# Two-layer encoder trunk on one core: the half of a step's projection pieces that stood between its scores and its transpositions is listed behind the transpositions

## The chip, the core and the metric

The kernel runs on one core of a Trainium2 chip. The metric is the device time of one execution in microseconds. Three runs of the kernel before gave 2654.55, 2655.66 and 2656.12 us; their median, 2655.66 us, is the time before. Lower is better. A difference is called faster or slower here if it is more than 0.2% of that, some 5.3 us.

The engines in the profile are PE (matrix multiplication), PEld (its loading of the stationary operand), DVE (vector), ACT (scalar and activation functions), POOL (a second, slower vector engine) and SP, which only issues transfers (SPq in a timeline).

## What is computed

One sequence of 2048 positions with 1024 channels goes through a gated layer A and then an attention layer B. Only layer B is touched. Its query block of 64 positions sees its own block of 64 and the eight before it:

```python
q, z = jnp.split(h @ w_qz, 2, axis=-1)
...
sc = jnp.einsum('bqhd,bkhd->bhqk', qc, kc).astype(jnp.float32) + bias
...
p = jax.nn.softmax(sc, axis=-1).astype(vc.dtype)
return jnp.einsum('bhqk,bkhd->bqhd', p, vc)
...
return (o * jax.nn.silu(z)) @ w_out
```

There are 16 heads of 64 channels, and `k` and `v` are projections of the same stream. The residual is added to the result and a last normalisation follows.

## The kernel before

**Staging.** The first part of the program (to about 1536 us of the profile) is layer A and the projection of all values; it is not touched. The second part is layer B. Positions are cut into four tiles of 512 (`t` from 0 to 3), and heads are taken two at a time (`p` from 0 to 7), so there are 32 pairs. For each pair there are eight steps `u`: two heads with four query blocks of 128 rows each.

**What a step of attention does.** `score(t, p, u)` multiplies a query block with up to 640 keys on PE into the one two-bank tile of the pool `bss` (names `s`); DVE adds the bias, keeps the maximum and moves the sum out of that tile (L1406); ACT takes the exponential and the row sum (L1413); DVE takes the reciprocal (L1416); POOL scales the row (L1417). `flip(t, p, u)` transposes the scaled block on PE, up to five 128x128 blocks, into the one two-bank tile of the pool `ptr` (names `tp`); ACT copies it out as the high part (L1437), and DVE subtracts that from the same tile to get the low part (L1438). Both go into `pt`, of which there is one buffer. `value(t, p, hd)` multiplies the four transposed blocks of a head with the values (16 matmuls named `pv`, 8 in tile 0). Scores run ahead: in step `u` the scores of step `u + 2` are made, in the last two steps those of the next pair.

**Projection pieces.** Between these stand pieces of other PE work, which a generator `ahead(t, p)` hands out: the projections of queries, keys and gate for the next pair (`project`, `values`, `gate`), and from tile 1 on pieces of the output projection of the tile before (`outs`). All multiplications with weights run as three matmuls, high by high, low by high and high by low, at L111, L112 and L113. A piece is three of them; they are named `pj` for the projections and `bo` for the output projection. Both accumulate in the four-buffer pool `pmm`, which `value` uses too. Each projection of 24 matmuls needs its weights split by ACT (L228) and DVE (L229) ahead of it. `steps_of(t, p)` says how many pieces a pair has (16 to 32, with 24 to 30 from tile 1 on in most pairs), and `total * (2 * u + 1) // per` and `total * (2 * u + 2) // per` say how many are to have been handed out by the middle and by the end of step `u`.

**What sets the order.** The listed order is not the order of the instructions on the engines. A scheduler goes through the list and may take a later instruction first when by its own account an earlier one isn't ready; each engine then runs its queue in the order so made, and waits on semaphores. What stands in a queue is therefore read from the built program.

The loop of a step, lines 1909 to 1931, reads in short:

```python
for u in range(8):
    score(...)                                 # of two steps later
    take(gen, upto - done)                     # pieces, first half
    if u == 4: value(t, p, 0)
    elif u == 0 and before: value(*before, 1)
    flip(t, p, u)
    ...                                        # drains, stores, squares
    take(gen, upto - done)                     # pieces, second half
```

Of the kernel before, what the change touches and what calls it, by code (L numbers as in the profile page):

```python
# [33 lines left out]
def trunk_kernel(  # L34
# [224 lines left out]
    def o_right(t):  # L259
        def right(ph):  # L260
            if (t, ph) in o_early:
                return o_early.pop((t, ph))
            out = []
            for q in range(2):
                name = f"bo{t}_{ph}_{q}"
                w = [w_tile(f"w{i}_{name}") for i in "hl"]
                if ph in o_raw:
                    raw = raw_w(1, f"raw_{name}")
                    nc.sync.dma_start(raw[:], wb_out[o_raw[ph]][q])
                    hi = split_in(raw, *w)  # L270
                    if (ph, q) == (1, 1):
                        on_beat(hi)
                else:
                    for i in range(2):
                        nc.sync.dma_start(w[i][:].bitcast(F32), ows[ph, q][:, i, :])
                out.append(w)
            return out
        return right
# [1000 lines left out]
    with ExitStack() as bctx:  # L1279
# [16 lines left out]
        def half_tile(tag, name, bufs, dtype=F32):  # L1296
            return sb.tile([P, 512], dtype, tag=tag, name=name, bufs=bufs)
# [17 lines left out]
        def project(t, p):  # L1315
            for acc in one(t, p, 1):
                yield
            for hd in range(2):
                qh = sb.tile([P, T], F32R, tag="Q", name=f"Qh{t}_{p}_{hd}", bufs=8)
                ql = sb.tile([P, T], F32R, tag="Q", name=f"Ql{t}_{p}_{hd}", bufs=8)  # L1320
                r, r2 = halves(hd)
                nc.scalar.mul(qh[r, :], acc[r, :], 0.125)
                nc.vector.scalar_tensor_tensor(
                    ql[r, :], acc[r, :], 0.125, qh[r, :].bitcast(F32),
                    op0=ALU.mult, op1=ALU.subtract,
                )
                for x_ in (qh, ql):
                    nc.sync.dma_start(x_[r2, :].bitcast(F32), x_[r, :].bitcast(F32))
                qt[t, p, hd] = (qh, ql)
            for acc in one(t, p, 0):  # L1330
                yield
            for hd in range(2):
                r, r2 = halves(hd)
                kx = sb.tile([P, 2 * T], F32R, tag="K", name=f"K{t}_{p}_{hd}", bufs=4)
                nc.scalar.copy(kx[r, T:], acc[r, :])
                nc.vector.tensor_tensor(
                    kx[r2, T:], acc[r, :], kx[r, T:].bitcast(F32), op=ALU.subtract
                )
                if t + 1 < NT:
                    k_store = (khd[t][p][hd], kx[:, T:].bitcast(F32))  # L1340
                    if held:
                        kept.append(k_store)
                    else:
                        nc.sync.dma_start(*k_store)
                if t > 0:
                    nc.sync.dma_start(kx[:, :T].bitcast(F32), khd[t - 1][p][hd])
                kt[t, p, hd] = kx
            if not held:
                keep_all()
# [116 lines left out]
        def drain_all():  # L1466
            while drains:
                drains.pop(0)()
# [28 lines left out]
        def square_all(every=False):  # L1497
            if every:
                squares.extend(young)
                young.clear()  # L1500
            while squares:
                on_beat(squares.pop(0)())
            squares.extend(young)
            young.clear()
# [9 lines left out]
        def send_all():  # L1514
            while owed_out:
                on_beat(nc.sync.dma_start(*owed_out.pop(0)))
# [39 lines left out]
        def last_open():  # L1556
            big = [sh.tile([P, 4, 1024], F32, tag=f"h{i}", name=f"A_h{i}") for i in "hl"]
            for i, n in enumerate(("00", "10", "01", "11", "s3", "s1", "s2", "s4")):
                la[n] = big[i // 4][:, i % 4, :]
            for c, k in ((0, 4), (1, 2)):  # L1560
                for r in range(2):
                    nc.sync.dma_start(
                        la[f"{r}{c}"][:, : k * 256],
                        ogd[NT - 1][:, r, 4 * c : 4 * c + k].rearrange("p k j s -> p (k j s)"),
                    )

            def third():
                for cs in (slice(0, 512), slice(512, 1024)):
                    on_beat(tg(la["s3"][:, cs], la["00"][:, cs], la["10"][:, cs], op=sub))

            def all_of(cs):
                for f_ in last_sums(cs):
                    f_()

            return [lambda: None, third] + last_sums(slice(0, 512)) + [lambda: all_of(slice(512, 768))]
# [250 lines left out]
        def take(gen, n):  # L1826
            for _ in range(n):
                if next(gen, gen) is gen:
                    return

        def run(gen):
            for _ in gen:
                pass
# [16 lines left out]
        def ahead(t, p):  # L1850

            if t > 1 and p == 0:
                next(outs[t - 1])
            if p + 1 < NPAIR:
                yield from project(t, p + 1)
                values(t, p + 1)
                for q in GATES[t][p]:
                    yield from gate(t, q)
                if (t, p) == (1, 4):
                    next(outs[0])  # L1860
                yield from some(outs[t - 1], SHARE[t][p])
            elif t + 1 < NT:
                yield from some(outs[t - 1], SHARE[t][p])
                yield from border(t)
                yield from project(t + 1, 0)
                values(t + 1, 0)
                yield from gate(t + 1, 0)
            else:
                yield from some(outs[t - 1], SHARE[t][p] - 6)
                last_first()  # L1870
                yield from some(outs[t - 1], 6)
                yield from some(outs[t], 13)

        def steps_of(t, p):
            n = 24
            if p + 1 < NPAIR:
                n = 16 + 8 * len(GATES[t][p])
            elif t + 1 == NT:
                n = 13
            return n + SHARE[t][p]  # L1880

        load_bias(0, 0)
        gen = project(0, 0)
# [9 lines left out]
        for t in range(NT):  # L1893
            for p in range(NPAIR):
                gen = ahead(t, p) if t + p else first
                total = steps_of(t, p) - (0 if t + p else 8)
                per = 11 if p + 1 == NPAIR and t + 1 < NT else 16
                todo = []
                if t + 1 == NT and p + 1 == NPAIR:
                    o_early[t - 1, 3] = o_right(t - 1)(3)  # L1900
                    todo = last_open()
                if t == 1 and p < 4:
                    todo = o_sums(p, lambda n: half_tile("C", n, 4), lambda n: half_tile(
                        "S", n, 4, F32R
                    ))
                if (t, p) == (0, 3):
                    nc.sync.dma_start(gf[:], fin_g.partition_broadcast(P))
                done = 0
                for u in range(8):
                    if u < 6:  # L1910
                        score(t, p, u + 2)
                    elif p + 1 < NPAIR or t + 1 < NT:
                        score(t + (p + 1) // NPAIR, (p + 1) % NPAIR, u - 6)
                    upto = total * (2 * u + 1) // per
                    take(gen, upto - done)
                    done = max(done, upto)
                    if u == 4:
                        value(t, p, 0)
                    elif u == 0 and before:
                        value(*before, 1)  # L1920
                    flip(t, p, u)
                    drain_all()
                    send_all()
                    square_all()
                    if u and finals:
                        finals.pop(0)()
                    if todo:
                        todo.pop(0)()
                    upto = total * (2 * u + 2) // per
                    take(gen, upto - done)  # L1930
                    done = max(done, upto)
                if t + 1 < NT or p + 1 < NPAIR:
                    run(gen)
                before = t, p
# [61 lines left out]
```

## Time and profile before

| | |
|---|---|
| median of three runs | 2655.66 us |
| span of the profiled execution, first to last instruction | 2652.0 us |
| run median less span | 3.7 us |
| PE busy in the span | 2608.0 us (98%) |
| DVE busy | 1885.1 us (71%) |
| ACT busy | 1303.2 us (49%) |
| POOL busy | 897.2 us (34%) |
| mean granted PE clock | 0.996 |

The profiled execution is known by its span alone; no time of its own around the span is listed for it, so the distance of 3.7 us between span and median is taken as what lies around it. A row of a group reads: line, engine, operation, output and inputs, shape and count, then busy time and the mean time of one, then the idle time of the engine just ahead of these instructions and what ended most of it. A row of a timeline reads: start and length in us, engine, line, operation, output and inputs, and in brackets the idle time ahead with what ended it. A row of stretches gives for each engine its busy time, then the granted clock of PE, the share of the transfer engines, and their rate.

### The profile page before, as it was taken

What the parts mean: (1) busy time and instruction counts of PE and PEld (TensorE: products, weight loads), DVE (VectorE), ACT (ScalarE), POOL (GpSimd) and SP (SyncE); (2) the same over time, 40 slices, a digit from 0 to 9 for tenths busy, and PEclk for the clock granted to TensorE, in tenths of its full rate; (3) what the DMA queues carried; (4) which work ended last, traced back from release to release, by engine and by line L of the source; (5) the groups of instructions that cost most, each with busy time, mean ns of one, the idle gap of its engine ahead of it and who ended that gap; (6) DMA issues with size and microseconds to landing.
All of it is one profiled execution on the core that took longest, in us unless ns stands there. A gap on an engine that the chain in (4) does not pass through costs nothing. (4 is left out here: it accounts for less than half of the span.)

```text
span 2652.0 us, 37980 instructions
## 1 busy us (share of the span) xinstructions
PE 2608.0 (98%) x12960; PEld 2181.4 (82%) x12960; DVE 1885.1 (71%) x2944; ACT 1303.2 (49%) x2303; POOL 897.2 (34%) x874
## 2 busy tenths in 40 slices
PE   8999999999999999999989999999999999999997
PEld 7888888888888888888878878888888888888886
DVE  5655676865767667757767767777778777877677
ACT  5422243442533434343356456666666655666564
POOL 3611334142152322203234434344332232332245
PEclk9999999999999999999999999999999999999999
DMA  7898998989989869967776597778787666875667
GB/s 286 313 344 329 346 370 323 323 323 338 330 302 313 308 233 324 331 206 270 280 251 214 186 280 229 231 245 263 252 270 254 226 204 224 255 230 161 195 224 251
DMA packets 273856, 718.72 MB, mean 271 GB/s; under 512 B 28800, under 2 KB 68736, under 8 KB 273664
## 3 DMA queue, kind: packets, MB, share of 16 engines
q1 hardware_dynamic: 273664, 716.31, 78.4%
q8 instruction: 103, 1.69, 0.3%
q14 instruction: 89, 0.73, 0.1%
HBM read 531.12 MB, written 174.59 MB: 266 GB/s over the span
## 5 line engine op out<-in xcount | busy, mean ns | idle before, releaser
L111 PE MATMUL P<-T,S 128*128 128x512 f32 x1248 | 496.2, 398 | 2.1 <-ACT S L434 2.1
L112 PE MATMUL P<-T,S 128*128 128x512 f32 x1248 | 488.2, 391 | 1.1 <-DVE T L437 1.1
L113 PE MATMUL P<-T,S 128*128 128x512 f32 x1248 | 488.6, 391 | 0.0
L1417 POOL TENSOR_SCALAR pr<-pr,sl 128x640 f32<-128x640 f32 (+4 forms) x256 | 209.7, 819 | 530.4 <-DVE sl L1416 445.2
L111 PE MATMUL pj<-hh_b,wh_b 128*128 128x512 f32 x768 | 320.4, 417 | 0.0
L113 PE MATMUL pj<-hh_b,wl_b 128*128 128x512 f32 x768 | 305.0, 397 | 1.2 <-DVE wl_b L229 1.1
L112 PE MATMUL pj<-hl_b,wh_b 128*128 128x512 f32 x768 | 303.4, 395 | 0.1
L1413 ACT ACTIVATE pr<-pr,nm 128x640 f32<-128x640 f32 (+4 forms) x256 | 195.5, 764 | 188.1 <-DVE nm L1406 186.6
L113 PEld LDWEIGHTS P<-T,S 128*128 128x128 f32 x1248 | 234.9, 188 | 50.5
L111 PEld LDWEIGHTS P<-T,S 128*128 128x128 f32 x1248 | 235.5, 189 | 46.9 <-ACT S L434 2.3
L112 PEld LDWEIGHTS P<-T,S 128*128 128x128 f32 x1248 | 235.6, 189 | 46.1 <-DVE T L437 1.3
L1438 DVE TENSOR_TENSOR pt<-tp,pt 128x640 fp32r<-128x640 f32 (+4 forms) x256 | 188.4, 736 | 43.7 <-ACT pt L1437 41.1
L1406 DVE CUSTOM_DVE_ANT_0 pr<-s,bias 128x640 f32<-128x640 f32 (+4 forms) x256 | 187.9, 734 | 35.7 <-PE s L1398 29.8
L1437 ACT CAST pt<-tp 128x640 fp32r<-128x640 f32 (+4 forms) x256 | 159.0, 621 | 54.0 <-PE tp L1433 49.8
L1433 PE MATMUL tp<-ident,pr 128*128 128x128 f32 x1120 | 166.7, 275 | 8.6 <-DVE pt L1438 7.3
L113 PEld LDWEIGHTS pj<-hh_b,wl_b 128*128 128x128 f32 x768 | 144.7, 188 | 36.4 <-DVE wl_b L229 3.8
L1433 PEld LDWEIGHTS tp<-ident,pr 128*128 128x128 f32 x1120 | 130.7, 140 | 43.3 <-issue 13.7
L111 PEld LDWEIGHTS pj<-hh_b,wh_b 128*128 128x128 f32 x768 | 145.8, 190 | 18.1 <-ACT wh_b L228 1.6
L1458 PEld LDWEIGHTS pv<-pt,V 128*128 128x128 f32 x896 | 143.3, 189 | 20.8 <-DVE pt L1438 3.9
L112 PEld LDWEIGHTS pj<-hl_b,wh_b 128*128 128x128 f32 x768 | 145.8, 190 | 17.1 <-DVE hl_b L186 0.6
L1458 PE MATMUL pv<-pt,V 128*128 128x256 f32 (+3 forms) x896 | 154.5, 320 | 2.2 <-ACT pt L1437 1.1
L229 DVE TENSOR_TENSOR wl_b<-raw_b,wh_b 128x1024 fp32r<-128x1024 f32 x96 | 120.4, 1255 | 28.5 <-ACT wh_b L228 27.8
(294 smaller groups left out, 5725.9 us busy)
## 6 DMA issues: line engine op xcount, KB each, us to landing
S<-hsd SPq DMA_DIRECT2D x288, 512.0 KB, 5.3
rw<-in_w_a SPq DMA_DIRECT2D x108, 512.0 KB, 6.3
A<-ytd SPq DMA_DIRECT2D x72, 512.0 KB, 5.7
raw_b<-wk SPq DMA_DIRECT2D x72, 512.0 KB, 4.3
hsd<-S SPq DMA_DIRECT2D x56, 512.0 KB, 4.9
V<-vhd SPq DMA_DIRECT2D x56, 512.0 KB, 5.4
bias<-reld SPq DMA_DIRECT2D x64, 320.0 KB, 4.2
va<-vd SPq DMA_DIRECT2D x32, 512.0 KB, 5.5
```

Source lines behind the costliest of these rows:

```text
L111: first = mm(ps, lh, rh, start=first, stop=False)
L112: mm(ps, lh, rl, start=False, stop=False)
L113: mm(ps, ll, rh, start=False, stop=last)
L229: tv(wl[:], raw[:], wh[:].bitcast(F32), op=sub)
L1406: nc.vector.tensor_tensor_reduce(out=pr[:, c0:].rearrange("p (a b) -> p a b", a=nseg), in0=ps[:, :nseg, :w], in1=bias[:, c0:].rearrange("p ...
L1413: nc.scalar.activation(pr[:, c0:], pr[:, c0:], AF.Exp, scale=-1.0, bias=nm[:], accum_out=sl[:])
L1417: nc.gpsimd.tensor_scalar(pr[:, c0:], pr[:, c0:], sl[:], 1.0, op0=ALU.mult, op1=ALU.mult)
L1433: ins = tpose(tp[:, b, :], pr[:, b * P : (b + 1) * P], ident[:])
L1437: nc.scalar.copy(oh, tp[:, b0:5, :].rearrange("p a b -> p (a b)"))
L1438: nc.vector.tensor_tensor(pt[:, 2560 + o + b0 * P : 2560 + o + 640], tp[:, b0:5, :].rearrange("p a b -> p (a b)"), oh.bitcast(F32), op=ALU ...
L1458: mm(po[:, q0 * P : q1 * P], vtl[t, p][:, i, hs], rhs, start=(i == blocks[0] and j == 0), stop=(i == 7 and j == 1),)
```

## The change

Three lines go. The first of the two calls of `take` in a step is left out, so nothing is handed out between the scores and the transpositions; the call at the end of the step, which is unchanged, then hands out all that is due by the end of the step. The number of pieces by the end of each step stays the same.

```diff
                     elif p + 1 < NPAIR or t + 1 < NT:
                         score(t + (p + 1) // NPAIR, (p + 1) % NPAIR, u - 6)
-                    upto = total * (2 * u + 1) // per
-                    take(gen, upto - done)
-                    done = max(done, upto)
                     if u == 4:
                         value(t, p, 0)
                     elif u == 0 and before:
                         value(*before, 1)
                     flip(t, p, u)
```

No instruction is added or removed; 3522 of some 12960 matmuls stand at another place of PE's queue, all of them in layer B. Three places show how.

**PE, tile 2, heads 4 and 5, the middle of a pair.** `s_4_3` are the scores of head 4, block 3; `tp_4_1` is the transposition of head 4, block 1; `pj_3_1` is the query projection of the next pair. Before:

```order
L1398 MATMUL s_4_3_20110<-K_2_0_19853,Qh_2_0_19766 128x320 x2
L1398 MATMUL s_4_3_20110<-K_2_0_19853,Ql_2_0_19767 128x320 x2
L111 MATMUL pj_3_1_20067<-hh_b,wh_b_3_1_20062 128x512
L112 MATMUL pj_3_1_20067<-hl_b,wh_b_3_1_20062 128x512
L113 MATMUL pj_3_1_20067<-hh_b,wl_b_3_1_20063 128x512
L111 MATMUL pj_3_1_20067<-hh_b,wh_b_3_1_20062 128x512
L112 MATMUL pj_3_1_20067<-hl_b,wh_b_3_1_20062 128x512
L113 MATMUL pj_3_1_20067<-hh_b,wl_b_3_1_20063 128x512
L1433 MATMUL tp_4_1_20128<-ident,pr_4_1_19995 128x128 x5
```

The same place of the changed program:

```order
L1398 MATMUL s_4_3_20110<-K_2_0_19883,Qh_2_0_19774 128x320 x2
L1398 MATMUL s_4_3_20110<-K_2_0_19883,Ql_2_0_19775 128x320 x2
L1433 MATMUL tp_4_1_20122<-ident,pr_4_1_19995 128x128 x5
L111 MATMUL pj_3_1_20100<-hh_b,wh_b_3_1_20095 128x512
L112 MATMUL pj_3_1_20100<-hl_b,wh_b_3_1_20095 128x512
L113 MATMUL pj_3_1_20100<-hh_b,wl_b_3_1_20096 128x512
```

The transposition moved ahead of six projection matmuls, to the scores; behind it now stand twelve in a run.

**PE, the border of tile 1 and tile 2.** `tp_15_3` is the last transposition of tile 1, `pv_15` the product of that head with its values, `s_0_1` and `s_0_2` are scores of tile 2. Before:

```order
L1398 MATMUL s_0_1_19211<-K_0_0_19143,Ql_0_0_19045 128x320 x2
L1433 MATMUL tp_15_3_19226<-ident,pr_15_3_19113 128x128 x5
L111 MATMUL pj_1_1_19267<-hh_b,wh_b_1_1_19262 128x512
L112 MATMUL pj_1_1_19267<-hl_b,wh_b_1_1_19262 128x512
L113 MATMUL pj_1_1_19267<-hh_b,wl_b_1_1_19263 128x512
L111 MATMUL pj_1_1_19267<-hh_b,wh_b_1_1_19262 128x512
L112 MATMUL pj_1_1_19267<-hl_b,wh_b_1_1_19262 128x512
L1398 MATMUL s_0_2_19238<-K_0_0_19143,Qh_0_0_19044 128x320 x2
L1398 MATMUL s_0_2_19238<-K_0_0_19143,Ql_0_0_19045 128x320 x2
L1458 MATMUL pv_15_19271<-pt_15_19086,V_7_18522 128x512
```

In the changed program:

```order
L1398 MATMUL s_0_1_19211<-K_0_0_19137,Ql_0_0_19075 128x320 x2
L1433 MATMUL tp_15_3_19223<-ident,pr_15_3_19113 128x128 x5
L1458 MATMUL pv_15_19246<-pt_15_19054,V_7_18522 128x512
L111 MATMUL pj_1_1_19296<-hh_b,wh_b_1_1_19291 128x512
L1398 MATMUL s_0_2_19234<-K_0_0_19137,Qh_0_0_19074 128x320 x2
L1398 MATMUL s_0_2_19234<-K_0_0_19137,Ql_0_0_19075 128x320 x2
L112 MATMUL pj_1_1_19296<-hl_b,wh_b_1_1_19291 128x512
L1458 MATMUL pv_15_19246<-pt_15_19054,V_7_18522 128x512 x3
```

The first `pv` matmul follows the transposition at once, where five projection matmuls and a block of scores stood between them.

**DVE, the same pair of tile 2 as at first.** `nm` and `pr` are written by the reduction that empties the tile of scores (L1406, two rows each), `pt_4` with `tp_4_2` by the subtraction that empties the transposition's tile (L1438), `wl_b_3_0` is the low part of the key weights (L229). Before:

```order
L1406 ISA pr_5_0_20147,nm_5_0_20148<-s_5_0_20142,bias_5_19986 128x640
L1406 ISA nm_5_0_20148 128x1
L229 TENSOR_TENSOR wl_b_3_0_20171<-raw_b_3_0_20169,wh_b_3_0_20170 128x1024
L1416 RECIPROCAL sl_5_0_20149<-sl_5_0_20149 128x1
L1406 ISA pr_5_1_20202,nm_5_1_20203<-s_5_1_20197,bias_5_19986 128x640
L1406 ISA nm_5_1_20203 128x1
L1323 SCALAR_TENSOR_TENSOR Ql_3_0_20158<-pj_3_1_20067,Qh_3_0_20157 64x512
L1438 TENSOR_TENSOR pt_4_20088<-tp_4_2_20179,pt_4_20088 128x640
```

In the changed program:

```order
L1406 ISA pr_5_0_20147,nm_5_0_20148<-s_5_0_20142,bias_5_19986 128x640
L1406 ISA nm_5_0_20148 128x1
L1438 TENSOR_TENSOR pt_4_20078<-tp_4_2_20154,pt_4_20078 128x640
L1406 ISA pr_5_1_20202,nm_5_1_20203<-s_5_1_20197,bias_5_19986 128x640
L1406 ISA nm_5_1_20203 128x1
L1416 RECIPROCAL sl_5_0_20149<-sl_5_0_20149 128x1
L1323 SCALAR_TENSOR_TENSOR Ql_3_0_20166<-pj_3_1_20100,Qh_3_0_20165 64x512
L229 TENSOR_TENSOR wl_b_3_0_20179<-raw_b_3_0_20177,wh_b_3_0_20178 128x1024
```

The subtraction moved ahead of the weight split and of a query split, and stands right behind the reduction.

## The prediction

> **What bounds the kernel now.** I read the totals of the engines first, then four stretches of the span, then PE's waits in the stretches that the change touches, then its groups of instructions. The totals:
>
> ```profile
> span 2652.0 us, 37980 instructions
> PE 2608.0 (98%) x12960; PEld 2181.4 (82%) x12960; DVE 1885.1 (71%) x2944; ACT 1303.2 (49%) x2303; POOL 897.2 (34%) x874
> ```
>
> PE is busy in 98% of the span. The stretches are the part that is not touched, the entry into the attention, its steady part and the end; the columns behind the length are PE, PEld, DVE, ACT and POOL, then PE's granted clock.
>
> ```profile
> 0.00:1536.00 1536.00, 1516.94 (x7130) 1260.76 (x7131) 1047.90 (x1353) 624.69 (x1034) 497.71 (x363) 1.00 0.83 298
> 1536.00:1596.00 60.00, 55.93 (x265) 44.31 (x265) 38.17 (x100) 34.09 (x78) 24.79 (x38) 0.94 0.86 273
> 1596.00:2570.00 974.00, 968.81 (x5247) 823.47 (x5245) 732.36 (x1385) 604.16 (x1114) 329.82 (x436) 1.00 0.72 230
> 2570.00:2652.00 82.00, 66.35 (x323) 52.90 (x321) 66.65 (x109) 40.23 (x80) 44.88 (x38) 0.96 0.73 258
> ```
>
> In the steady part PE idles 974.00 - 968.81 = 5.2 us. In the entry it is 4.1 us, in the end stretch 15.7 us. DVE is busy for 75% of the steady part (732.36 of 974), so it has room on average. PE's waits there, as total, times and longest:
>
> ```profile
> PE tp L1433 <- DVE pt L1438: 3.7, 7, 0.9
> PE pj L113 <- DVE wl_b L229: 0.6, 2, 0.3
> PE pv L1458 <- DVE pt L1438: 0.2, 1, 0.2
> ```
>
> Seven transpositions of 183 waited for the subtraction that empties the tile of the transposition before. No scores waited. The end stretch has more of the same, and two waits of scores for the reduction:
>
> ```profile
> PE tp L1433 <- DVE pt L1438: 3.6, 5, 1.1
> ...
> PE s L1398 <- DVE nm L1406: 1.1, 2, 0.7
> PE pv L1458 <- DVE pt L1438: 0.4, 1, 0.4
> ```
>
> So PE's own work sets the time, and the waits that an order can remove in the steady part are a few microseconds in all. The groups that take part, in the steady part:
>
> ```profile
> L1433 PE MATMUL tp<-ident,pr 128*128 128x128 f32 x1037 | 152.8, 274 | 3.9 <-DVE pt L1438 3.7
> L1406 DVE CUSTOM_DVE_ANT_0 pr<-s,bias 128x640 f32<-128x640 f32 x186 | 152.2, 818 | 26.8 <-PE s L1398 21.9 <-POOL pr L1417 1.4 <-POOL bias L1379 1.0
> L1438 DVE TENSOR_TENSOR pt<-tp,pt 128x640 fp32r<-128x640 f32 x183 | 150.1, 820 | 36.8 <-ACT pt L1437 35.2
> L1437 ACT CAST pt<-tp 128x640 fp32r<-128x640 f32 x183 | 125.8, 687 | 34.9 <-PE tp L1433 31.7 <-PE pv L1458 1.0
> L229 DVE TENSOR_TENSOR wl_b<-raw_b,wh_b 128x1024 fp32r<-128x1024 f32 x86 | 108.2, 1259 | 21.6 <-ACT wh_b L228 20.9
> ```
>
> **The change, part by part.** *PE's own work.* Nothing is added or removed, and by the order of the built programs the first 6661 instructions of PE are the same. The work itself costs 0. What moves is the distance between instructions that share a tile. This is how the present distances pay:
>
> ```profile
> 2022.42 0.71 PE L1433 MATMUL tp<-ident,pr 128*128 128x128 f32 x5
> ...
> 2023.20 0.39 PE L112 MATMUL pj<-hl_b,wh_b 128*128 128x512 f32 x1
> 2023.43 0.39 PE L113 MATMUL pj<-hh_b,wl_b 128*128 128x512 f32 x1
> ...
> 2024.06 0.69 ACT L1437 CAST pt<-tp 128x640 fp32r<-128x640 f32 x1
> 2024.19 1.23 DVE L229 TENSOR_TENSOR wl_b<-raw_b,wh_b 128x1024 fp32r<-128x1024 f32 x1 [0.27 <-ACT wh_b L228]
> 2024.36 0.46 PE L1398 MATMUL s<-K,Qh 128*128 128x320 f32 x2
> ...
> 2024.94 0.39 PE L111 MATMUL pj<-hh_b,wh_b 128*128 128x512 f32 x1
> ...
> 2025.34 0.82 DVE L1438 TENSOR_TENSOR pt<-tp,pt 128x640 fp32r<-128x640 f32 x1
> ```
>
> A projection matmul takes 2023.43 - 2023.20 = 0.23 us of PE, a block of scores 2024.94 - 2024.36 = 0.58 us. The transposition ended at 2023.13 and its tile came free at 2026.16, 3.0 us later, with a weight split ahead of the subtraction on DVE. Without one, copy and subtraction are 0.69 + 0.82 = 1.5 us.
>
> *Transpositions behind each other.* From PE's order, each matmul counted at its time above, I took the PE work between consecutive transpositions of tiles 1 to 3. Under 2.4 us lie 7 of them before and 13 in the changed program; with six or fewer projection matmuls between, 1 before and 16 after. The present waits are 3.7 / 7 = 0.53 us each, so six more of them give 6 x 0.53 = **+3.2 us**. Bounds: 0, if the subtraction always stands first in DVE's queue (as in the place shown in the change), and 15 x 1.26 = 18.9 us, if each new close pair has a weight split ahead of it. I take the value by the row of the present waits.
>
> *Waits of today that go.* In DVE's order the work between the attention operation before and the subtraction falls from 1.27 to 0.79 us on average, and subtractions with over 1 us of it from 129 to 74 of 256, by 43%. Taken off the 3.9 us of L1438 in the steady part this is **-1.7 us**; bounds 0 and -8.3, all waits for L1438 in the steady part, the end and the entry (0.45 there, in the timeline below).
>
> *Scores behind each other.* Those with six or fewer projection matmuls between go from 14 to 19. Ahead of the reduction DVE's other work grows from 0.50 to 0.99 us on average. None of the 14 waits in the steady part; in the end two wait, 1.1 / 2 = 0.55 us each. I take one such wait, **+0.55 us**, between 0 and 5 x 0.55 = 2.75.
>
> *The product behind its last transposition.* At the border of tile 1 and 2 the 5 x 0.23 + 0.58 = 1.7 us between the two vanish. The nearest row is the same situation at the end of the first pair, with the only case of it today:
>
> ```profile
> 1588.92 0.50 PE L1458 MATMUL pv<-pt,V 128*128 128x512 f32 x1 [1.10 <-ACT pt L1437]
> 1589.87 1.74 PE L1458 MATMUL pv<-pt,V 128*128 128x512 f32 x7 [0.45 <-DVE pt L1438]
> ...
> 1585.00:1596.00 11.00, 9.45 (x40) 7.50 (x39) 5.88 (x13) 4.49 (x11) 5.10 (x5) 0.84 0.77 260
> ```
>
> 1.10 + 0.45 = 1.55, so **+1.5 us**; bounds 0 and twice that, since a second place (third pair of tile 2) has 0.5 us of PE work left, while all such places with under 1.5 us fall from 6 to 4.
>
> *Pieces that come later.* Half of a step's pieces move behind a transposition, with the weight splits (L228, L229) and weight loads that belong to them; on SP 389 and on POOL 111 instructions move, by a few places each. The number due by the end of a step is unchanged, so the queries and keys of the next pair are ready in the same step. The longest wait for them today is at the entry:
>
> ```profile
> PE s L1398 <- DMA Qh<-Qh: 1.4, 1, 1.4
> ```
>
> I cost it at 0; what hides it is the rest of the step, about twelve projection matmuls, 12 x 0.23 = 2.8 us. If that cover went, one wait of 1.4 us would come in some pairs; the upper bound is one in each of ten pairs, 14 us, and a gain of at most the 1.4 now seen. Weight splits that come later: 0.6 us today, 0 to 0.6 more, taken as 0.
>
> **Sum.** 3.2 - 1.7 + 0.55 + 1.5 = +3.55 us. The profiled execution spans 2652.0 us, and the median of the runs is 2655.66, 3.7 above. So the span becomes 2655.6 and the time 2655.6 + 3.7 = **2659 us**, +0.13%. A measurement of this kernel can tell about 0.2%, 5.3 us, from no change; this lies inside.
>
> **The rivals.** *The clustered evictions meet on DVE (slower).* Scores and transposition now stand together (the scores directly ahead in 145 of 256 cases, 3 before), so the reduction and the subtraction of one step fall due together, and each of the next step waits behind the other. This decides from the point at which a transposition's tile takes 2.7 us to come free and a scores' tile 2.3 us; the timeline above shows 3.0 with a split in the way. What the PE work in between then lacks, summed over tiles 1 to 3, grows from 6.1 to 12.4 us for the transpositions and from 9.7 to 15.8 for the scores: 6.3 + 6.1 = +12.4, time 2668. Against it: only 3.7 of the 6.1 and none of the 9.7 are waited for today.
>
> *Waits slow PE's clock as well (slower).* After the two waits at 1588.92 and 1589.87 the granted clock over 11 us was 0.84, that is 11 x 0.16 = 1.76 us lost; the steady part shows 1.00 with single waits of up to 0.9. So two waits close together, 1.5 us in 2, cost as much again in clock. Three such spells are +5.3, on the forecast 2664; five on top of the first rival, 8.8, give 2677.
>
> [...]
>
> *The subtractions are freed (faster).* With the split behind them, all waits for L1438 go: 3.7 + 0.2 + 3.6 + 0.4 + 0.45 = 8.3, time 2647.4. For it: the 43% above, and that no close pair of the new order has a split ahead of its subtraction. Against it: the end stretch, with 4.0 of the 8.3, has few projection pieces left to reorder, and closer transpositions spend what is gained.
>
> *The change doesn't do what it says.* The scheduler might sort the pieces back between scores and transposition. In 111 of 256 cases the scores don't come directly ahead, so it does so in part; were it the whole, 2655.7.
>
> **How the numbers follow.** The forecast with its neighbours (sum near zero, pieces sorted back, one clock spell) holds 0.5, all within 2650.4 and 2661, which is *same*. The meeting evictions have 0.22 and the clock spells 0.15, both above 2661: slower 0.37. The freed subtractions have 0.13: faster. Each term of the sum by its upper bound would give more than 2677, but no two of them share the same splits. The range is 2648 to 2677: below it lies the removal of all waits, above it more than the slower rivals together.
>
> **What would show it.** Right: the first 1536 us stay as they are; in the steady part PE's busy time stays at 968 to 970 us, the waits of `tp` for L1438 are 4 to 7 us, a wait of `pv` of over 1 us stands near 1964 us, and scores wait for L1406 once or twice. The first rival would show 6 us or more of waits of `s` for L1406 and 9 or more of `tp`; the clock rival a granted clock under 0.98 in some slices between 1596 and 2570; the third no row of `tp` for L1438. Scores or projections that wait for a DMA in the steady part would make the step "pieces that come later" wrong.

## The result, and the profile after

The changed kernel takes 2676.00 us (median of 5 runs, 2674.76 to 2676.44) against 2654.61 us of the kernel before (5 runs). The ratio is 1.0077, with a 95% interval of 1.0064 to 1.0089: slower by 21 us. The time lies in the range that was given, near its upper end, and 17 us above the forecast of 2659, which stood for "no change".

The totals of the changed kernel, and five stretches of its span (untouched part, tile 0, tile 1, tiles 2 and 3, end; columns as before):

```profile
span 2673.0 us, 37961 instructions
PE 2609.5 (98%) x12960; PEld 2185.2 (82%) x12960; DVE 1898.0 (71%) x2944; ACT 1302.7 (49%) x2303; POOL 906.5 (34%) x874
```

```profile
0.00:1536.00 1536.00, 1517.19 (x7132) 1260.11 (x7132) 1047.77 (x1353) 624.64 (x1034) 497.63 (x363) 1.00 0.84 298
1536.00:1745.00 209.00, 197.32 (x984) 159.90 (x984) 143.90 (x346) 124.72 (x275) 78.32 (x120) 0.99 0.73 234
1745.00:2040.00 295.00, 287.07 (x1551) 244.26 (x1550) 229.35 (x397) 184.12 (x329) 114.02 (x129) 0.99 0.77 249
2040.00:2592.00 552.00, 545.45 (x2997) 471.04 (x2996) 415.38 (x746) 331.81 (x592) 175.34 (x228) 1.00 0.68 215
2592.00:2673.00 81.00, 62.51 (x303) 49.89 (x301) 61.62 (x105) 37.43 (x75) 41.15 (x36) 0.97 0.72 249
```

PE's busy time grew by 1.5 us, the span by 21.0: nearly all of the loss is idle time of PE. It idles 209.00 - 197.32 = 11.7 us in tile 0 and 7.9 in tile 1. The stretches of the kernel before in which the same work is done show 4.5 and 1.9 us:

```profile
1536.00:1738.00 202.00, 197.53 (x988) 161.13 (x987) 142.63 (x345) 125.42 (x274) 78.42 (x120) 0.98 0.77 243
1738.00:2019.00 281.00, 279.13 (x1527) 238.08 (x1526) 220.01 (x394) 182.05 (x326) 107.68 (x128) 1.00 0.80 261
```

PE's waits in the changed kernel between 1596 and 2592 us, the stretch that corresponds to the steady part of before, as total, times and longest:

```profile
PE tp L1433 <- DVE pt L1438: 15.7, 16, 2.3
PE bo L112 <- DMA wl_bo<-ows: 1.0, 2, 0.8
PE s L1398 <- DVE nm L1406: 0.8, 2, 0.5
PE pv L1458 <- ACT pt L1437: 0.8, 1, 0.8
```

The first row was 3.7 us in 7 waits. There are 9 more, and the mean of one is 15.7 / 16 = 0.98 us instead of 0.53.

To see where the loss arises, I counted the matmuls of each trace at their pitch (0.231 us for 512 columns and in proportion for fewer, as 0.146 for the 320 of a block of scores, and 0.109 for a transposed block) and compared the times at which each kernel had done the work that the changed kernel has done at the time in the head of the column. The figures are good to about 1 us, since the kernels list the work in different orders.

| kernel, behind the kernel before by us | start of layer B (1536) | end of tile 0 (1745) | end of tile 1 (2036) | end of tile 2 (2326) | last matmul |
|---|---|---|---|---|---|
| changed | -0.5 | 7.3 | 16.8 | 19.0 | 20.5 |
| change in tile 0 alone | 0.4 | 6.5 | 7.1 | 7.5 | 7.1 |
| change in tile 1 alone | 1.6 | 0.4 | 9.8 | 10.3 | 10.4 |
| changed, gain multiplication a mark earlier | 1.1 | 28.3 | 35.8 | 38.7 | 38.2 |
| changed, splits tied | 3.9 | 5.9 | 12.5 | 12.7 | 10.8 |
| changed, no sums of weights | 5.4 | 12.9 | 15.9 | 18.0 | 20.1 |
| before, gain multiplication a mark later | 1.5 | 10.7 | 12.2 | 12.8 | 13.2 |

What a tile costs is the difference of two neighbouring columns. The first column is the lateness that a traced execution brings from the part that no kernel here touches. In the changed kernel tile 0 costs 7.8 us and tile 1 costs 9.5; tiles 2 and 3 cost 2.2 and 1.5. In tile 0 the loss is one wait in each of six pairs, always at the same step. The fourth of them, with the rows of every engine that take part, from the timeline of the changed kernel:

```profile
1655.16 0.59 POOL L1417 TENSOR_SCALAR pr<-pr,sl 128x384 f32<-128x384 f32 x1 [1.97 <-PE tp L1433]
...
1655.71 1.90 POOL L213 TENSOR_TENSOR raw_b<-raw_b,bg 128x1024 f32<-128x1024 f32 x1
...
1657.41 0.38 PE L1433 MATMUL tp<-ident,pr 128*128 128x128 f32 x2
...
1657.64 1.05 ACT L228 CAST wh_b<-raw_b 128x1024 fp32r<-128x1024 f32 x1 [1.78 <-POOL raw_b L213]
...
1658.72 1.23 DVE L229 TENSOR_TENSOR wl_b<-raw_b,wh_b 128x1024 fp32r<-128x1024 f32 x1 [2.24 <-ACT wh_b L228]
...
1659.87 0.68 DVE L1406 CUSTOM_DVE_ANT_0 pr<-s,bias 128x512 f32<-128x512 f32 x1
...
1660.47 0.42 DVE L1438 TENSOR_TENSOR pt<-tp,pt 128x256 fp32r<-128x256 f32 x1
...
1661.04 0.52 PE L1433 MATMUL tp<-ident,pr 128*128 128x128 f32 x3 [1.21 <-DVE pt L1438]
```

And the same split in the timeline of the kernel before:

```profile
1650.76 1.90 POOL L213 TENSOR_TENSOR raw_b<-raw_b,bg 128x1024 f32<-128x1024 f32 x1
...
1652.77 0.59 POOL L1417 TENSOR_SCALAR pr<-pr,sl 128x384 f32<-128x384 f32 x1
...
1653.78 1.23 DVE L229 TENSOR_TENSOR wl_b<-raw_b,wh_b 128x1024 fp32r<-128x1024 f32 x1 [1.18 <-ACT wh_b L228]
...
1654.92 0.28 DVE L1438 TENSOR_TENSOR pt<-tp,pt 128x128 fp32r<-128x128 f32 x1
```

Read from the end: the transposition waits 1.21 us for the subtraction, whose copy had been done since 1658.97. DVE stood idle for 2.24 us, not for lack of work but because the next row of its queue, the weight split L229, waited for ACT, which waited for POOL's gain multiplication L213. The reduction and the subtraction behind it could not pass. In the kernel before POOL did the multiplication ahead of a row scaling, now it stands behind one that itself waited 1.97 us, by the profile for a transposition; the split falls in front of the two-block subtraction instead of the one-block one. The weights themselves are in no hurry: by the order of the program their first use comes two transpositions after the one that waits.

In tile 1 three waits of 1.3 us and one of 2.3 also stand behind a split. The first of them, again from the timeline:

```profile
1783.21 0.73 PE L1433 MATMUL tp<-ident,pr 128*128 128x128 f32 x5
...
1783.77 3.00 POOL L376 TENSOR_TENSOR wo<-wo,wo 128x512 f32<-128x512 f32 x2
...
1785.54 2.31 DVE L229 TENSOR_TENSOR wl_b<-raw_b,wh_b 128x1024 fp32r<-128x1024 f32 x1
...
1787.88 0.82 DVE L1438 TENSOR_TENSOR pt<-tp,pt 128x640 fp32r<-128x640 f32 x1
...
1788.86 0.74 PE L1433 MATMUL tp<-ident,pr 128*128 128x128 f32 x5 [1.32 <-DVE pt L1438]
```

Here the split waits for nothing but lasts 2.31 us, beside POOL's sums of the output weights. At the fourth place, 1929.97, the split lasts 2.30 us beside another POOL operation, L1531 (`A<-A,A`).

### The profile page after: what moved, and what is told of

Read it like the earlier page. It is cut to its first block, busy times and chain, and to the rows that moved or that the text cites. A ratio compares the mean times of both kernels' runs of the same rounds, so it can differ in the third digit from the quotient of the medians.

```text
span 2673.0 us, 37961 instructions
## 1 busy us (share of the span) xinstructions
PE 2609.5 (98%) x12960; PEld 2185.2 (82%) x12960; DVE 1898.0 (71%) x2944; ACT 1302.7 (49%) x2303; POOL 906.5 (34%) x874
## 5 line engine op out<-in xcount | busy, mean ns | idle before, releaser
L1417 POOL TENSOR_SCALAR pr<-pr,sl 128x640 f32<-128x640 f32 (+4 forms) x256 | 215.6, 842 | 566.8 <-DVE sl L1416 459.5
L1406 DVE CUSTOM_DVE_ANT_0 pr<-s,bias 128x640 f32<-128x640 f32 (+4 forms) x256 | 188.2, 735 | 68.1 <-PE s L1398 55.6
L1438 DVE TENSOR_TENSOR pt<-tp,pt 128x640 fp32r<-128x640 f32 (+4 forms) x256 | 188.7, 737 | 35.7 <-ACT pt L1437 32.9
L229 DVE TENSOR_TENSOR wl_b<-raw_b,wh_b 128x1024 fp32r<-128x1024 f32 x96 | 125.6, 1309 | 30.9 <-ACT wh_b L228 29.3
```

Of the source, the lines that this page charges most:

```text
L229: tv(wl[:], raw[:], wh[:].bitcast(F32), op=sub)
L1406: nc.vector.tensor_tensor_reduce(out=pr[:, c0:].rearrange("p (a b) -> p a b", a=nseg), in0=ps[:, :nseg, :w], in1=bias[:, c0:].rearrange("p ...
L1417: nc.gpsimd.tensor_scalar(pr[:, c0:], pr[:, c0:], sl[:], 1.0, op0=ALU.mult, op1=ALU.mult)
L1438: nc.vector.tensor_tensor(pt[:, 2560 + o + b0 * P : 2560 + o + 640], tp[:, b0:5, :].rearrange("p a b -> p (a b)"), oh.bitcast(F32), op=ALU ...
```

## The experiments

I held two theories. **Late weight split**: what costs is where the split of a weight stands on DVE against the evictions. **Clustered evictions**, the rival of the prediction: scores and transposition side by side make the reduction and the subtraction collide.

**Where the loss is.** The change in one tile only, in the others the first `take` as before:

```diff
+                    if t > 0:          # second kernel: if t != 1
+                        upto = total * (2 * u + 1) // per
+                        take(gen, upto - done)
+                        done = max(done, upto)
                     if u == 4:
```

> The change in tile 0 alone; tiles 1 to 3 keep their first half of pieces ahead of the transposition. Theory 'late weight split' (the change sends the gain multiplication of a weight, L213 on POOL, one row scaling later; the split L229 on DVE then holds up the reduction and the subtraction behind it, and once a pair a transposition waits): tile 0 has six such waits of 1.2 us each, so about 7 to 8 us above before, 2662 to 2663, with the six waits in the trace. Rival 'clustered evictions' (scores and transposition side by side make reduction and subtraction collide everywhere): the loss of 21 us is spread by the size of the evictions, and tile 0 with its small blocks has less than a quarter of it, at most 5 us: 2656 to 2660.

> The change in tile 1 alone. Theory 'late weight split': tile 1 shows three waits of 1.3 us and one of 2.3 us, each behind a split that lasts 2.3 us instead of 1.2, and one stretch of 10 us at a clock of 0.83 behind the longest: 6.3 + 1.7 us, and some 2 us of smaller ones, so 2662 to 2665. Rival 'clustered evictions': tiles 1 to 3 share the loss alike, 5 to 7 us, 2660 to 2662, with its waits spread over many steps, none at a place of its own.

Measured: 1.0037 (1.0024 to 1.0049) for tile 0 and 1.0035 (1.0021 to 1.0050) for tile 1. Together 0.72%, of 0.77%: the two tiles carry the loss. The trace of the first has the six waits, 1.17 to 1.40 us each, that of the second the four, 1.32 to 2.31. So they belong to the place, not to the chance of a run.

**The split moved alone, first try.** In tile 0 the gain multiplication is tied to the projections' marks; the number says how many back:

```diff
-            paced_by_pj(scaled(raw, (bg if c else kg)[:, :, :]), 3)
+            paced_by_pj(scaled(raw, (bg if c else kg)[:, :, :]), 4)
```

> The changed kernel with one number altered: the gain multiplication L213 in tile 0 is tied to a mark of the projections one earlier (the fourth last instead of the third last), so that the weight split comes earlier on DVE while scores and transpositions stay side by side. Theory 'late weight split': the six waits of 1.2 us in tile 0 go, 7 us less, 2669. Rival 'clustered evictions': nothing that clusters has changed, 2676 within 2 us.

Measured: 2694.57 us, 1.0148 (1.0133 to 1.0163). Both expectations fell. The six waits did go, but the chain stood in a worse place. PE's waits in tile 0, and one of the places:

```profile
PE pv L1458 <- ACT pt L1437: 12.2, 7, 2.2
PE s L1398 <- DVE nm L1406: 7.4, 11, 1.5
```

```profile
1637.44 1.05 ACT L228 CAST wh_b<-raw_b 128x1024 fp32r<-128x1024 f32 x1 [2.29 <-POOL raw_b L213]
...
1639.76 0.59 ACT L1437 CAST pt<-tp 128x512 fp32r<-128x512 f32 x1
...
1640.40 0.51 PE L1458 MATMUL pv<-pt,V 128*128 128x512 f32 x1 [2.09 <-ACT pt L1437]
```

In the first view are total, count and longest; in the second, the timeline. Now ACT's half of the split held up the copy that the product with the values waits for, and DVE's half the reductions. The clustering is hardly different: scores stand directly ahead of a transposition 133 times in this trace and 145 times in that of the changed kernel. Yet one number in the place of the split is worth 18 us more, of which some 5 us go with a slower clock: 0.91 from 1600 to 1620 and from 1660 to 1680 and 0.96 from 1700 to 1740, where the changed kernel has 1.00, so 1.8 + 1.8 + 1.6 = 5.2 (see the last section). That "earlier is better" was wrong; that the place of the chain decides was not.

**The split tied behind the evictions.** Each split in layer B may not pass the copy and the subtraction of the transposition listed three before:

```diff
         hi = nc.scalar.copy(wh[:], raw[:])
-        tv(wl[:], raw[:], wh[:].bitcast(F32), op=sub)
+        hold_back(hi, 0)        # order only: behind copy [-3] on ACT
+        hold_back(tv(wl[:], raw[:], wh[:].bitcast(F32), op=sub), 1)   # behind subtraction [-3] on DVE
```

> The changed kernel with one tie added on ACT and on DVE: the two instructions of a weight split in layer B (L228, L229) may not come ahead of the copy and the subtraction of the transposition listed three before, so in tile 0 the split comes behind the subtraction that it held up, and still some steps ahead of its first use. Scores and transpositions stand as in the changed kernel. Theory 'late weight split': the six waits of 1.2 us in tile 0 and the waits of 1.3, 1.3, 1.3 and 2.3 us in tile 1 go, 7.3 + 6.3 us and the clock spell of 1.7 us, against new small ones: 2660 to 2664. Rival 'clustered evictions': nothing that clusters has changed, 2674 to 2678. Should it be worse than 2678, as with the pacing altered, the split in its new place holds up something else and the theory of the place is too simple.

> The kernel before with the same tie of the weight splits. Control: theory 'late weight split' says that the kernel before has no such waits in tiles 0 and 1, so the tie has little to gain there: 2653 to 2658. If it gains as much here as in the changed kernel (10 us or more), what it cures isn't what the change brought.

Measured: 2664.04 us, 1.0028 (1.0016 to 1.0040), for the changed kernel, and 0.9996 (0.9987 to 1.0005) for the kernel before. With scores directly ahead of a transposition 162 times in the trace, 12 of the 21 us come back; the kernel before gains nothing. In tile 0 no transposition waits for the subtraction any more; what is left there, with 11 lines more above it in the program (L1409 are the scores, L1417 the reduction):

```profile
PE s L1409 <- DVE nm L1417: 2.7, 7, 0.8
PE s L1409 <- DMA Qh<-Qh: 1.9, 1, 1.9
```

In the traces tile 0 costs 2.0 us instead of 7.8. Tile 1 gained less, 6.6 instead of 9.5 us: the wait beside `A<-A,A` stayed with 2.0 us, and four of 0.8 to 0.9 took the place of the three. Of the gain in tile 1, 1.7 us is a spell of a slower clock that did not come this time: the granted clock from 1745 to 2040 is 1.00, in the changed kernel 0.99.

**POOL beside the split.** First the sums were listed later in the pair, then left out (the second kernel lacks the sums of weights in the output projection):

```diff
-                    if todo:
-                        todo.pop(0)()
+                    for _ in range((0, 0, 1, 1, 1, 1, 2, 2)[u] if t == 1 else 1):
+                        if todo:
+                            todo.pop(0)()
```

> The changed kernel, with POOL's sums of the output weights in tile 1 (L376, 1.3 to 1.5 us each) listed from step 2 on instead of from step 0, so that they don't run beside the split at the start of a pair. Theory 'late weight split', with POOL making it longer: the splits at the three waiting places of tile 1 take 1.2 instead of 2.3 us and the waits of 1.3 us shrink by 1.1 each: 3.2 us less, 2673. Rival 'clustered evictions': 2676 within 1.5 us. A third reading, in which the split is slow for another reason than POOL: the same waits remain at 1.3 us with the split at 2.3.

> The changed kernel without POOL's four sums of the output weights per pair in the first four pairs of tile 1 (L376 and L380 left out, so the sums of weights are missing from the output projection). The order on DVE at the waiting places is the same, row for row. Theory 'late weight split': the splits there run beside POOL's L376 and take 2.31 us; without it they take 1.2, and the three waits of 1.3 us behind them shrink to about 0.25 each: 3.2 us less, 2673, and up to 2 more where ACT and DVE wait for those sums. Rival 'the place alone counts, not POOL': the splits stay at 2.3 us and the time at 2676.

Measured: 1.0076 (1.0061 to 1.0091) with the sums later, no gain. The three waits went from the start of the pair to its end, one of them 0.85 and two over 2.2 us. There, as the timeline reads, ACT and DVE stood still for a weight that came late from memory, ahead of the copy and subtraction of the next transposition:

```profile
1831.77 1.05 ACT L228 CAST wh_b<-raw_b 128x1024 fp32r<-128x1024 f32 x1 [3.28 <-DMA raw_b<-wk]
...
1832.85 1.23 DVE L229 TENSOR_TENSOR wl_b<-raw_b,wh_b 128x1024 fp32r<-128x1024 f32 x1 [3.98 <-ACT wh_b L228]
```

Without the sums: 2670.61 us, 1.0051 (1.0035 to 1.0066), 5.4 us less than the changed kernel, where 3 to 5 were expected; the intervals of the two ratios just touch. The trace is plainer: tile 1 costs 3.0 us instead of 9.5, and at the three places the split lasts 1.22 us and no transposition waits, with the same order on DVE. The fourth wait, beside `A<-A,A`, stayed with 2.15 us. (The 20.1 us at the end of its row in the table hold the 5.4 us that this execution had lost before layer B.) At the first of the three places:

```profile
1790.29 1.22 DVE L229 TENSOR_TENSOR wl_b<-raw_b,wh_b 128x1024 fp32r<-128x1024 f32 x1
...
1791.54 0.83 DVE L1438 TENSOR_TENSOR pt<-tp,pt 128x640 fp32r<-128x640 f32 x1
```

**Both together.**

> The changed kernel with the tie of the weight splits (the run before of that kind: 2664) and without POOL's sums in tile 1. What is left in tile 1 there are four waits of 0.8 to 0.9 us behind a subtraction of the sums' copies, which itself waits for POOL and ACT, and one of 2.0 us. Theory 'a slow chain over POOL and ACT in front of the eviction on DVE' (the weight split is one such chain, the sums are another): the four waits go, 3.4 us, and some of the waits of scores: 2659 to 2661. Rival 'what is left is the clustering itself': 2664 within 1.5 us.

Measured: 2659.62 us, 1.0016 (1.0007 to 1.0025), the time expected but not the way: the four waits stayed, 0.75 to 0.83 us each. One of them:

```profile
1764.61 0.69 DVE L382 TENSOR_TENSOR so_6l<-wo,so_6h 128x512 fp32r<-128x512 f32 x1 [0.91 <-ACT so_6h L381]
...
1765.97 0.82 DVE L1449 TENSOR_TENSOR pt<-tp,pt 128x640 fp32r<-128x640 f32 x1 [0.41 <-ACT pt L1448]
...
1766.94 0.74 PE L1444 MATMUL tp<-ident,pr 128*128 128x128 f32 x5 [0.77 <-DVE pt L1449]
```

DVE waits ahead of the low part of those weights for ACT's high part, not for POOL. The pattern is the same, the chain starts one engine later than I had written. What else made this run faster than the one with the ties alone I did not settle.

**The same chain without the clustering.** If the place of the split decides, the kernel before must lose as well when its chain comes later:

```diff
-            paced_by_pj(scaled(raw, (bg if c else kg)[:, :, :]), 3)
+            paced_by_pj(scaled(raw, (bg if c else kg)[:, :, :]), 2)
```

> The kernel before, with the gain multiplication L213 in tile 0 tied to a mark of the projections one later, so that the weight split of a pair falls behind POOL's next row scaling and on DVE ahead of the subtraction of the transposition two steps later; pieces, scores and transpositions are listed as before. Theory 'late weight split': waits of about 1 us once a pair in tile 0 appear with no clustering at all, 3 to 8 us: 2658 to 2663. Rival 'clustered evictions': nothing clusters, 2655 within 2 us.

Measured: 2667.28 us, 1.0035 (1.0023 to 1.0047), 9 us by the ratio and 12 by the medians, more than the 3 to 8 expected, with every piece listed as before. PE's waits from 1536 to 1760 us:

```profile
PE pv L1458 <- DVE pt L1438: 3.3, 6, 0.5
PE s L1398 <- DVE nm L1406: 3.0, 1, 3.0
PE pv L1458 <- ACT pt L1437: 2.6, 6, 1.8
PE tp L1433 <- DVE pt L1438: 1.9, 3, 1.2
```

Six pairs wait again, this time mostly at the product with the values. The 3.0 us are one wait ahead of the first pair, where the split stands in front of a reduction.

**The end and the opposite.** The last pair as before; all pieces of a step ahead of its transposition (`2 * u + 2` in the first `take`, restored); and this except in the last pair.

> The changed kernel with the last pair of tile 3 as before (first half of its pieces ahead of the transposition). By the trace the last pair lost 3.4 us, with a wait of 2.6 us for POOL (A_hl) and one of 1.3 us for a reciprocal that the kernel before does not have. Theory 'late weight split' has nothing to do with these; if they are the change's own, a second cause at the end, 2672 to 2673; if they are only the earlier lateness carried on, 2676.

> The opposite change: all pieces due by the end of a step are handed out between its scores and its transposition, none behind. Theory 'late weight split': what counts is where a split stands against the next eviction, so the sign isn't fixed by the distance of scores and transposition; with the longest cover ahead of each transposition 2650 to 2660. Rival 'clustered evictions': the scores then stand directly behind the transposition of the step before, as close as in the changed kernel, so the same 15 to 25 us are lost: 2670 to 2680.

> All pieces of a step ahead of its transposition, except in the last pair, where half stay behind as in the kernel before. By the traces, all-ahead was 2.4 us in front of the kernel before until the last pair and lost it there: if that is so, 2652 to 2653, 0.1% under the kernel before, which may not be told from no change; if the lost time at the end was only caught up late, 2655 to 2656.

Measured: 1.0061 (1.0040 to 1.0082) for the last pair as before, not to be told from the changed kernel; its profile has the same span, 2673.1 us. The wait of 2.6 us for POOL at the end of the changed kernel is gone there, but one of 2.4 for L1438 came. A second cause at the end is not seen; three runs with this interval could not exclude one of 3 us. All ahead gave 1.0003 (0.9994 to 1.0012), except in the last pair 0.9997 (0.9988 to 1.0006): both are no change, and the second is no gain to keep. Moving the transpositions the other way, behind all of their step's pieces, costs nothing. Clustering by itself should have cost there too, since the next scores then follow the transposition directly: 219 times in the trace of all ahead, 3 times in that of the changed kernel.

## Why the prediction was right and wrong

**Right.** What bounds the kernel: the first 1536 us did not change (1517.19 us of PE against 1516.94), PE's work stayed, and all that could be gained was a few microseconds. The scores' waits came as sized: 0.8 us between 1596 and 2592 where 0.55 was said. The wait of the product at the border of tile 1 and 2 came, with 0.78 us instead of 1.5, and at 2048 us; the 1964 of the prediction was a place in PE's queue without its idle times. Pieces that come later did not make queries or keys late; two matmuls of the output projection did wait for weights from memory, 1.0 us in all, which the prediction had at nothing. Behind one wait the clock was lower too; the timeline's row and the stretch behind it:

```profile
1929.97 0.74 PE L1433 MATMUL tp<-ident,pr 128*128 128x128 f32 x5 [2.31 <-DVE pt L1438]
```

```profile
1930.90:1934.30 3.40, 3.40 (x10) 2.62 (x9) 0.98 (x2) 1.35 (x3) 1.24 (x2) 0.50 0.62 196
```

3.4 x 0.50 = 1.7 us are lost. The kernel before has such a spell behind the two waits at 1588.92, 0.50 from 1590.42 to 1593.83, and there the changed kernel has none. So as a whole the clock rival did not come: the mean clock is 0.997 against 0.996.

**Wrong.** The step that failed is "Weight splits that come later: 0.6 us today, 0 to 0.6 more, taken as 0". It priced a late split by the projection that uses it. That projection still has time; what pays is the eviction queued behind the split on DVE or ACT. In the runs this was worth some 7 us in tile 0 (six waits of 1.2) and, with POOL beside it, 6 us in tile 1.

Two more steps hid it. "Transpositions behind each other" did name a split ahead of the subtraction, as its upper bound of 18.9 us, but took the mean of 0.53 us, which came from waits without such a chain. It counted tiles 1 to 3 alone and took a pair as close under 2.4 us of PE work. The number of new waits, nine for six, was near, but of the eleven waits of over 1 us ten stand elsewhere: six in tile 0, with nine projection matmuls between, 9 x 0.23 = 2.1 us, and four in tile 1 at pairs that seemed far enough apart, with thirteen and a block of scores, 13 x 0.23 + 0.58 = 3.6 us. There the tile came free late, 1660.89 - 1657.79 = 3.1 us after the transposition at the place shown of tile 0, 1788.70 - 1783.94 = 4.8 us at that of tile 1, because the 1.23 us of a split, which the prediction knew, come with the idle time ahead of it (2.24) or with POOL beside it (1.08 more). And "Waits of today that go", -1.7, took DVE's other work ahead of the subtraction as an average; by the prediction's own count the average falls, while the place that pays in each of these ten pairs got worse.

The slower rival had the sign and not the cause. Of its two marks one came, over 9 us of `tp` waits (15.7), and one did not, 6 us of `s` waits (0.8). Clustered evictions alone, with the splits tied, cost at most the 7 us (4 to 11 by the interval) that remain, and part of these is traced to other chains. Its 2668 was short of 2676; only the range reached that far. That is luck: the upper end of the range was clustering plus five spells of a slow clock, and neither brought the 21 us.

**Open.** Of the 9.5 us in tile 1 the waits on L1438 and the clock spell make 7.5 (6.8 + 1.7, less the 1.0 of before). The remaining 2 us, and the 6.6 us that tile 1 still costs with the splits tied, are not wholly assigned. Nor is it shown how much of the 7 us that remain with the ties is clustering.

## What to carry to other kernels

When an order changes, ask of every moved instruction not only who waits for its result but who is queued behind it, and whether its own inputs are ready when it gets to the front: here a low-priority chain over three engines cost nothing or 1.2 us a pair in tile 0, depending on which eviction it happened to precede. Averages over a stage hide this; go through one period of the loop and follow each in-order queue past the slowest chain. If the chain has slack, tie it behind the evictions, before judging the reordering itself.

## What the runs showed of the hardware

In layer B of the changed kernel, where the split on DVE and a POOL operation overlapped by 0.19 us or more, one of the two took longer in every case but one. The split of 128x1024 took 1.21 to 1.23 us alone and 2.31 to 2.33 at all four places where POOL's L376, a two-input operation, was running when it began; without L376 it took 1.22. In the rows above POOL's pair ends at 1783.77 + 3.00 = 1786.77, and the split at 1785.54 + 2.31 = 1787.85, 1.08 us later, about its own length. So the split looks as if it had started only when POOL was done, rather than having run at half speed; the cause was not shown. Alone, POOL was the slower of the two: L213, with two inputs of 128x1024 as the split has, took 1.90 us.

In this trace it made the difference who began first, and row scalings were among the POOL operations that did so. A split that began during a POOL operation took longer by what was left of that operation less some 0.15 us: 1.74 us with 0.67 left, 1.46 with 0.39, and 1.23, no longer, with 0.09. With 0.15 us or more left, it ended 1.07 to 1.09 us behind POOL's operation in 21 of 22 cases in layer B; the one beside an operation of 128x1 (L126) took 1.22. A split that began first, or within 0.01 us of the first, took 1.20 to 1.24 us, and it was POOL's operation that took longer: the row scaling below lasts 2.14 us, where others of its size take 0.80.

```profile
1764.21 1.21 DVE L229 TENSOR_TENSOR wl_b<-raw_b,wh_b 128x1024 fp32r<-128x1024 f32 x1
...
1764.46 2.14 POOL L1417 TENSOR_SCALAR pr<-pr,sl 128x640 f32<-128x640 f32 x1 [0.72 <-DVE sl L1416]
```

In layer B, up to PE's last matmul, the clock records of the two kernels' traces show 1.00 but for spells of 3.41 us at 0.50: at 1538.34 and 1930.87 in the changed kernel, at 1539.22 and 1590.42 in the kernel before. The 0.84 over 11 us of the prediction and the 1.7 us lost above are each one of them. They start whole multiples of 3.4133 us apart: 1930.87 - 1538.34 = 392.53 = 115 x 3.4133 in the changed kernel and 1590.42 - 1539.22 = 51.20 = 15 x 3.4133 in the kernel before. Cut into steps of that length, layer B of these traces has 1.55, 1.65, 1.90 and 2.31 us of idle PE in the steps ahead of the four spells and at most 1.47 in the others, but for one step with 1.82 us, at 2616.95 in the changed kernel, that no spell followed. The length of a wait alone does not sort the cases either: the wait of 2.31 us at 1929.97 was followed by a spell, and so were those of 1.10 and 0.45 us in the kernel before, but the wait of 2.15 us in the run without sums left the clock at 1.00 in every stretch between 1600 and 2500, and that of 2.0 us in the run with ties alone left it at 1.00 from 1745 to 2040. What decides was not shown. The waits of 1.2 us, 26 us apart, left the clock at 1.00 between 1600 and 1700.

```profile
1600.00:1700.00 100.00, 94.45 (x475) 76.14 (x474) 68.31 (x164) 58.10 (x130) 40.22 (x56) 1.00 0.67 215
```
